# Attention values with column halves stationary, sinks as a score column, and a written TensorE order in the mixer

## The chip, the core and the metric
One core of a Trainium2 chip runs the whole program in one launch. The engines each have a queue of their own, executed in order: TensorE (PE; PEld is its load of the stationary operand), VectorE (DVE), ScalarE (ACT), GpSimd (POOL) and SyncE (SP, which issues most transfers). The metric is the device time of one execution in microseconds, the median over runs.

## What is computed
Two trunk layers over 384 tokens: 128 context tokens (block 0) and 256 latent tokens (blocks 1 and 2). A layer is a half-step SwiGLU, a mixer, and a second half-step SwiGLU. The mixer has four head groups behind one input projection: mLSTM, global attention (group B), windowed attention with sink logits (group C), and a Hyena long convolution; one output projection follows. The attention, cut from the reference:

```
def attn_probs(s, sink):
    if sink is None:
        return jax.nn.softmax(s, axis=-1)
    m = jnp.maximum(jnp.max(s, -1, keepdims=True), sink)
    e = jnp.exp(s - m)
    return e / (jnp.sum(e, -1, keepdims=True) + jnp.exp(sink - m))
...
    s = jnp.einsum('bqkgd,bmkd->bkgqm', qblk, k).astype(F32)
    p = attn_probs(s, sink)
    return jnp.einsum('bkgqm,bmkd->bqkgd', p.astype(v.dtype), v)
```

Each group has 4 query heads of 64 on 2 key heads (`kv`), two query heads (`g`) to a key head. Context queries see the 128 context keys, latent queries 128 cached keys and 256 of their own; group C masks the latent keys that lie further than 128 positions away and adds a sink logit to the softmax. The new context keys and values are outputs too.

## The kernel before
Activations lie feature-major (feature in the partition, 384 tokens in the free dimension). Every large product is exact to about float32 by three float32r matmuls (`prod3`, L235): high weights with high and low activations, low weights with high. Weights arrive by SP (`weights_load`, L219), ScalarE makes the high part (L231), VectorE the low one (L232), four buffers each. The order on each engine is chosen by the framework's planner from a cost model, by program order as priority; only the start of the kernel is written out (`manual_schedule`, L1391).

The mixer (L733) projects the mLSTM's queries and keys, then values, then group B and group C token-major (`tok_major`, L746), with the mLSTM's products between. Then comes the stage that the change touches:

- `attention(grp)` (L980): raw queries and keys are copied out of PSUM (L992), values too (L993). Per block in the order 1, 2, 0 they are normed (B, L1010 to L1012) or scaled (C, L1014 and L1015, on ScalarE), stored in `hat`, rotated (L1025 to L1027), transposed on TensorE (L1030) and copied to `qT` (L1031). `hat` of block 0 has one buffer (L1004) and is the source of the store of the new keys (L1017). The cached keys are transposed too (L999).
- `scores` (L1033): query block stationary, keys moving, the two key heads on partitions 0 to 63 and 64 to 127; cached and own keys are separate products; C adds a mask product in bfloat16 (L1053).
- softmax: maximum on VectorE (L1066), for C a minimum with the negated sink (L1068); exponential with its sum on ScalarE (L1070), for C another one for the sink (L1072) and an addition (L1073); reciprocal (L1074).
- the unnormalised probabilities are transposed (L1076), copied by VectorE (L1078), and are the stationary operand of the value product (L1083), with 64 columns of values moving. VectorE scales the result (L1084) into `ot`, which `to_cat` (L768) transposes back (L772) and splits into `ch` and `cl`, the high and low inputs of the output projection.
- `hyena_in` (L1110) makes three projections of 8 k-steps (24 matmuls) for each channel half m, then a short convolution on VectorE (L1131 to L1133). `hyena` (L1138) transposes (L1148), goes through a DFT (L594, L1159 to L1163) and back (L1169).
- the output projection (L1181): for each of two column halves q, four pairs of k-tiles, each with 4 x 2 x 3 matmuls.

In program order all of group B stands before group C, and that before Hyena; the planner moves Hyena's projections (`pdu`) forward into the attention. PSUM has two pools of four banks: `mm` for projections and `small` for the rest.

Of the kernel before, what the change touches and what calls it, by code (L numbers as in the profile page):

```python
# [9 lines left out]
F32 = mybir.dt.float32  # L10
# [7 lines left out]
P = 128  # L18
# [4 lines left out]
DEPTH = 2  # L23
# [67 lines left out]
def trunk_kernel(ctx: ExitStack, tc: tile.TileContext, I: dict, C: dict, O: list):  # L91
# [124 lines left out]
    def weights(src, nk, ncol, name):  # L216
        return weights_split(weights_load(src, nk, ncol, name), nk, ncol, name)

    def weights_load(src, nk, ncol, name):  # L219
# [485 lines left out]
    def mixer_constants():  # L705
# [12 lines left out]
        K["nsinks"] = const.tile([P, DEPTH, 4], F32, name="nsinks")  # L718
        tc.keep_in_program_order(V.tensor_scalar(out=K["nsinks"], in0=K["sinks"], scalar1=-1.0, scalar2=None, op0=ALU.mult))
# [13 lines left out]
    def mixer(l, K, nm, nxt, fill):  # L733
# [246 lines left out]
        def attention(grp):  # L980
            isB = grp == "B"
            pa = [mm(f"pa{b}") for b in range(3)]
            tok_major(pa, C_BQ if isB else C_CQ, f"{grp}{l}")
            kc = am.tile([P, 2 * HD], F32, tag="kc", name="kc")
            vc = am.tile([P, 2, HD], F32, tag="vc" + grp, name="vc")
            ksrc, vsrc = (I["cache_gattn_k"], I["cache_gattn_v"]) if isB else (I["cache_swa_k"], I["cache_swa_v"])
            nc.gpsimd.dma_start(out=kc, in_=ksrc[0, l].rearrange("t h d -> t (h d)"))
            nc.gpsimd.dma_start(out=vc, in_=vsrc[0, l])
            raw = [am.tile([P, 384], F32, tag="raw", bufs=3, name="raw") for b in range(3)]
            vt = am.tile([P, 3, 2, HD], F32, tag="vt" + grp, name="vt")  # L990
            for b in range(3):
                S.copy(raw[b], pa[b][:, 0:384])  # L992
                S.copy(vt[:, b], pa[b][:, 384:512].rearrange("p (h d) -> p h d", h=2))  # L993
            ko, vo = (5, 6) if isB else (7, 8)
            nc.scalar.dma_start(out=O[vo][0, l], in_=vt[:, 0])
            qT = am.tile([P, 3, NT], F32, tag="qT" + grp, name="qT")
            kcT = am.tile([P, P], F32, tag="kcT" + grp, name="kcT")
            pkc = small("pkc")
            T.transpose(pkc[:, :P], kc, ident)  # L999
            S.copy(kcT, pkc[:, :P])  # L1000
            if isB:
                rr = head_rstd(lambda b: raw[b], 6, "qn")
            for b in (1, 2, 0):
                hat = am.tile([P, 6, HD], F32, tag="hat" if b else "hat0", bufs=2 if b else 1, name="hat")  # L1004
                qv = hat[:, 0:4, :].rearrange("p (g kv) d -> p kv g d", g=2)
                rq = raw[b][:, 0:256].rearrange("p (kv g d) -> p kv g d", kv=2, g=2)
                rk = raw[b][:, 256:384].rearrange("p (h d) -> p h d", h=2)
                if isB:
                    rn = raw[b].rearrange("p (h d) -> p h d", h=6)
                    V.tensor_tensor(out=rn, in0=rn, in1=bc(rr[:, b, :].unsqueeze(2), [P, 6, HD]), op=ALU.mult)  # L1010
                    V.tensor_tensor(out=qv, in0=rq, in1=bc(K["gq"][:, l:l + 1, :].unsqueeze(1), [P, 2, 2, HD]), op=ALU.mult)
                    V.tensor_tensor(out=hat[:, 4:6, :], in0=rk, in1=bc(K["gk"][:, l:l + 1, :], [P, 2, HD]), op=ALU.mult)  # L1012
                else:
                    S.mul(qv, rq, 0.125)  # L1014
                    S.copy(hat[:, 4:6, :], rk)  # L1015
                if b == 0:
                    nc.gpsimd.dma_start(out=O[ko][0, l], in_=hat[:, 4:6, :])  # L1017
                else:
                    cosb = rope[:, b - 1, 0:1, :]
                    sinb = rope[:, b - 1, 1, :].rearrange("p (a h f) -> p a h f", a=2, h=2)  # L1020
                    t = am.tile([P, 6, HD], F32, tag="rt", bufs=2, name="rt")
                    hv = hat.rearrange("p n (a h f) -> p n a h f", a=2, h=2)
                    tv = t.rearrange("p n (a h f) -> p n a h f", a=2, h=2)
                    for hf in range(2):
                        V.tensor_tensor(out=tv[:, :, :, hf, :], in0=hv[:, :, :, 1 - hf, :], in1=bc(sinb[:, :, hf, :].unsqueeze(1), [P, 6, 2, 16]), op=ALU.mult)  # L1025
                    V.tensor_tensor(out=hat, in0=hat, in1=bc(cosb, [P, 6, HD]), op=ALU.mult)
                    V.tensor_tensor(out=hat, in0=hat, in1=t, op=ALU.add)  # L1027
                p = small("pqT")
                for j in range(3):
                    T.transpose(p[:, j * P:(j + 1) * P], hat[:, 2 * j:2 * j + 2, :].rearrange("p h d -> p (h d)"), ident)  # L1030
                S.copy(qT[:, :, b * P:(b + 1) * P], p[:, :NT].rearrange("p (j t) -> p j t", j=3))  # L1031
            ot = am.tile([P, 3, 256], F32, tag="ot", name="ot")
            def scores(b, g):  # L1033
                ss = [small("s") for _ in range(2)]

                def part(c0, n, key, start=True, stop=True):
                    for kv in range(2):
                        r = slice(kv * 64, kv * 64 + 64)
                        T.matmul(ss[kv][:, c0:c0 + n], lhsT=qT[r, g, b * P:(b + 1) * P], rhs=key(r), start=start, stop=stop)  # L1039

                own = lambda c0, n: (lambda r: qT[r, 2, c0:c0 + n])
                if b == 0:
                    part(0, P, own(0, P))
                    return ss
                part(0, P, lambda r: kcT[r, :])
                if isB:
                    part(P, 2 * P, own(P, 2 * P))
                    return ss
                near, far = (P, 2 * P) if b == 1 else (2 * P, P)
                part(near, P, own(near, P))  # L1050
                part(far, P, own(far, P), stop=False)
                for kv in range(2):
                    T.matmul(ss[kv][:, far:far + P], lhsT=K["ident16"], rhs=K["wmask"][:, (b - 1) * P:b * P], start=False, stop=True)  # L1053
                return ss

            for b in (1, 2, 0):
                nk = 1 if b == 0 else 3
                n = nk * P
                for g in range(2):
                    ss = scores(b, g)  # L1060
                    sts, pts = {}, {}
                    for kv, s in enumerate(ss):
# [4 lines left out]
                        if not isB:  # L1067
                            V.tensor_tensor(out=nmx, in0=nmx, in1=K["nsinks"][:, l, h:h + 1], op=ALU.min)  # L1068
# [411 lines left out]
```

## Time and profile before
| | us |
|---|---|
| median of three runs | 1672.38 |
| lowest and highest run | 1649.3, 1673.61 |
| the profiled execution | 1664.59 |
| its span, first to last instruction | 1662.8 |

The profile is of one execution: busy time and share of each engine, the span in 40 slices (a digit is a share in tenths, PEclk the TensorE clock granted by the throttle, in tenths of full speed), groups of instructions by line, waits, timelines. Times of a row count from the start of the span. A matmul's duration includes its way through the array, so that neighbours overlap; start to start says what one costs in a stream.

### The profile page before, as it was taken

The numbers are of one execution on the slowest core, as the hardware profiler recorded it, in microseconds if no ns is written. First come the engines' busy times: TensorE is split into PE (matmuls) and PEld (weight loads), VectorE is DVE, ScalarE is ACT, GpSimd is POOL, SyncE is SP. The second block draws the span as 40 slices with busy tenths as digits, with TensorE's granted clock in tenths as the row PEclk, the third lists the DMA queues.
The fourth block names the chain that finished last, engine by engine and source line by source line (L and its number), as shares of the span: only waits on it lengthen the run. The fifth ranks groups of instructions, "written<-read, shape, count | busy, mean of one in ns | idle before, by whom it ended". The sixth has DMA issues, their size and how long they took to land.

```text
span 1662.8 us, 25089 instructions
## 1 busy us (share of the span) xinstructions
PE 1621.3 (98%) x9145; PEld 1529.0 (92%) x9145; DVE 1272.1 (77%) x2564; ACT 761.0 (46%) x1771; POOL 240.9 (14%) x342
## 2 busy tenths in 40 slices
PE   7999999999989999999999999999999999999998
PEld 4789999997878999999999999999787899999997
DVE  5899997997858689996999977697785867444333
ACT  5534444458434464443546434345843446333331
POOL 2113222241010002221320211123101000000000
PEclk9999999999979999999999999999996999999999
DMA  9657757763431368766766774765343133444341
GB/s 309 203 156 244 225 183 242 220 179 104 128 63 59 102 189 242 240 185 199 216 207 192 240 210 135 243 211 146 103 131 59 53 108 115 127 127 127 114 133 58
DMA packets 235728, 271.23 MB, mean 163 GB/s; under 512 B 14239, under 2 KB 220287, under 8 KB 235604
## 3 DMA queue, kind: packets, MB, share of 16 engines
q1 hardware_dynamic: 223104, 248.67, 48.9%
q0 software_dynamic: 9472, 20.30, 4.9%
q10 hardware_dynamic: 3028, 0.64, 0.4%
q8 instruction: 72, 1.18, 0.3%
q14 instruction: 52, 0.43, 0.1%
HBM read 257.62 MB, written 3.57 MB: 157 GB/s over the span
## 4 chain that ended last, share of the span: by engine, by line
PE 75%; DVE 13%; issue 5%; DMA 4%; ACT 3%; POOL 0%; SPq 0%; DVEq 0%; ACTq 0%; POOLq 0%
PE pg L236 7%; PE pg L237 7%; PE pu L238 7%; PE pg L238 7%; PE pu L237 6%; PE pu L236 6%; DVE adacc L266 5%; PE pd L238 4%; PE pd L237 4%; PE pd L236 4%; PE s L1083 2%; PE s L1039 2%; PE pwo L238 1%; PE pwo L237 1%; PE pwo L236 1%
## 5 line engine op out<-in xcount | busy, mean ns | idle before, releaser
L266 DVE SCALAR_TENSOR_TENSOR adacc<-flat,sc,adacc 128x384 f32<-128x384 f32 (+1 forms) x602 | 353.0, 639 | 0.0
L290 POOL TENSOR_TENSOR adfold<-adacc,adfold 64x384 f32<-64x384 f32 (+1 forms) x86 | 122.3, 1422 | 149.2 <-DMA adfold<-adacc 146.8
L238 PE MATMUL pd<-ah,lo_db 128*128 128x384 f32 x352 | 119.2, 339 | 1.6 <-DVE lo_db L232 1.6
L238 PE MATMUL pd<-ah,lo_da 128*128 128x384 f32 x352 | 119.0, 338 | 1.7 <-DVE lo_da L232 1.7
L237 PE MATMUL pg<-wide,hi_gb 128*128 128x384 f32 (+1 forms) x352 | 119.6, 340 | 0.2
L236 PE MATMUL pg<-wide,hi_gb 128*128 128x384 f32 (+1 forms) x352 | 119.6, 341 | 0.0
L236 PE MATMUL pd<-ah,hi_da 128*128 128x384 f32 x352 | 119.5, 339 | 0.0
L236 PE MATMUL pd<-ah,hi_db 128*128 128x384 f32 x352 | 119.4, 339 | 0.0
L238 PE MATMUL pg<-wide,lo_gb 128*128 128x384 f32 (+1 forms) x352 | 118.9, 338 | 0.0
L237 PE MATMUL pd<-al,hi_db 128*128 128x384 f32 x352 | 118.9, 338 | 0.0
L237 PE MATMUL pu<-wide,hi_ub 128*128 128x384 f32 (+1 forms) x352 | 118.8, 338 | 0.0
L237 PE MATMUL pd<-al,hi_da 128*128 128x384 f32 x352 | 118.6, 337 | 0.0
L238 PE MATMUL pu<-wide,lo_ub 128*128 128x384 f32 (+1 forms) x352 | 118.5, 338 | 0.0
L236 PE MATMUL pu<-wide,hi_ub 128*128 128x384 f32 (+1 forms) x352 | 118.2, 337 | 0.0
L236 PE MATMUL pg<-wide,hi_ga 128*128 128x384 f32 (+1 forms) x328 | 112.8, 344 | 1.0 <-DVE sg L555 1.0
L236 PE MATMUL pu<-wide,hi_ua 128*128 128x384 f32 (+1 forms) x328 | 110.6, 338 | 2.7 <-DVE sg L555 2.7
L241 ACT CAST ah<-sg 128x384 fp32r<-128x384 f32 x88 | 45.2, 513 | 148.1 <-DVE sg L555 146.6
L237 PE MATMUL pg<-wide,hi_ga 128*128 128x384 f32 (+1 forms) x328 | 111.4, 340 | 0.0
L238 PE MATMUL pg<-wide,lo_ga 128*128 128x384 f32 (+1 forms) x328 | 111.3, 340 | 0.0
L237 PE MATMUL pu<-wide,hi_ua 128*128 128x384 f32 (+1 forms) x328 | 111.0, 338 | 0.0
L238 PE MATMUL pu<-wide,lo_ua 128*128 128x384 f32 (+1 forms) x328 | 110.8, 338 | 0.0
L232 DVE TENSOR_TENSOR lo_db<-st_db,hi_db 128x1024 fp32r<-128x1024 f32 (+1 forms) x48 | 54.4, 1133 | 64.2 <-ACT hi_db L231 64.2
(487 smaller groups left out, 4381.5 us busy)
## 6 DMA issues: line engine op xcount, KB each, us to landing
flat<-in_w_ada_dram SPq DMA_DIRECT2D x42, 1536.0 KB, 7.9
st_gb<-in_w_gate_dram SPq DMA_DIRECT2D x44, 512.0 KB, 3.8
st_ub<-in_w_up_dram SPq DMA_DIRECT2D x44, 512.0 KB, 4.7
st_ga<-in_w_gate_dram SPq DMA_DIRECT2D x41, 512.0 KB, 3.9
st_ua<-in_w_up_dram SPq DMA_DIRECT2D x41, 512.0 KB, 4.9
st_da<-in_w_down_dram SPq DMA_DIRECT2D x40, 512.0 KB, 5.3
st_db<-in_w_down_dram SPq DMA_DIRECT2D x40, 512.0 KB, 3.5
wst<-in_w_ada_dram SPq DMA_DIRECT2D x8, 1024.0 KB, 13.3
```

Source lines behind the costliest of these rows:

```text
L232: V.tensor_tensor(out=lo[:, :n], in0=st[:, :n], in1=hi[:, :n].bitcast(F32), op=ALU.subtract)]
L236: T.matmul(out, lhsT=lh, rhs=rh, start=start, stop=False)
L237: T.matmul(out, lhsT=lh, rhs=rl, start=False, stop=False)
L238: T.matmul(out, lhsT=ll, rhs=rh, start=False, stop=stop)
L241: S.copy(hi, src)
L266: last_step[0] = V.scalar_tensor_tensor(out=acc[:, s, :n * P], in0=w[:, k, :], scalar=sc[:, k, s:s + 1], in1=acc[:, s, :n * P], op0=ALU.mu ...
L290: G.tensor_tensor(out=fold[h, :c], in0=acc[h, s, :c], in1=fold[h, :c], op=ALU.add)
L1039: T.matmul(ss[kv][:, c0:c0 + n], lhsT=qT[r, g, b * P:(b + 1) * P], rhs=key(r), start=start, stop=stop)
L1083: T.matmul(s[:, NT:NT + HD], lhsT=pts[kv][:, j * P:(j + 1) * P], rhs=v, start=(j == 0), stop=(j == nk - 1))
```

## The change
The attention becomes a class `Group` with methods, and what TensorE executes from the last token-major projection to the end of the output projection stands in program order under `manual_schedule` for that engine alone; the other engines stay with the planner.

- Values: probabilities are normalised on ScalarE before they are transposed. The value product has 64 columns of values stationary and 128 columns of transposed probabilities moving; key head 0 writes the lower half of the output partitions, key head 1 the upper half. The result is feature-major, so `ot`, its scaling and `to_cat` of the two groups go; it is split at once. The rows of the output projection's weights for these groups are loaded in the order that this gives (`paired`, two transfers of 64 partitions).
- Sinks: one more column of the scores, made by a product of the identity with the sink column; maximum and sum then include it. `nsinks`, L1068, L1072 and L1073 go.
- Keys: queries, own keys and cached keys share one tile, so that a long step has one score product per key head instead of two or three. `hat` has three buffers for all blocks, and the context keys are stored from `ko` (B) or `raw` (C).
- Order: both groups are prepared first. Then a loop over 12 steps (group, block, query head) issues the scores of the next step, the transposes of this one, two k-steps of a Hyena projection (one for block 0), the values of this one, queries for four steps ahead, and again two k-steps. Hyena's first half runs inside these k-steps, its second half in fixed places of the output projection.
- Engines: of each pair of copies of probabilities one moves to ScalarE; so does the first term of the convolution.

```diff
-        nc.sync.dma_start(out=st[:, :n].rearrange("p (k f) -> p k f", k=nk), in_=src.rearrange("(k p) f -> p k f", p=P))
+        if paired:
+            for kv in range(2):
+                nc.sync.dma_start(out=out[kv * 64:kv * 64 + 64], in_=src.rearrange("(kv g d) f -> kv d g f", kv=2, g=2)[kv])
...
-                hat = am.tile([P, 6, HD], F32, tag="hat" if b else "hat0", bufs=2 if b else 1, name="hat")
+                    hat = am.tile([P, 6, HD], F32, tag="hat", bufs=3, name="hat")
...
+                    kh = hat[:, 4:6, :]
+                    if b == 0:
+                        kh = am.tile([P, 2, HD], F32, tag="ko", name="ko") if isB else rk
...
+            def queries(self, b):
+                p = mm("pqT")
...
+            def scores(self, b, g):
...
+                n = P if b == 0 else 3 * P
+                k0 = QW if b == 0 else QW + P
+                ss = [small("s") for _ in range(2)]
+                for kv in range(2):
+                    r = slice(kv * 64, kv * 64 + 64)
+                    T.matmul(ss[kv][:, 0:n], lhsT=qT[r, g * NT + b * P:g * NT + (b + 1) * P], rhs=qT[r, k0:k0 + n], start=True, stop=isB or b == 0)
+                if not isB:
...
+                    for kv in range(2):
+                        T.matmul(ss[kv][:, n:n + 1], lhsT=ident, rhs=K["sinks"][:, l, 2 * kv + g:2 * kv + g + 1], start=True, stop=True)
+                    n += 1
...
+                    V.tensor_reduce(out=nmx, in_=s[:, :n], axis=AX.X, op=ALU.max, negate=True)
+                    pe = am.tile([P, NT + 1], F32, tag="pe", bufs=2, name="pe")
+                    S.activation(out=pe[:, :n], in_=s[:, :n], func=AF.Exp, bias=nmx, accum_out=den)
+                    V.reciprocal(out=den, in_=den)
+                    n_ = P if b == 0 else 3 * P
+                    S.activation(out=pe[:, :n_], in_=pe[:, :n_], func=AF.Identity, scale=den)
...
+            def turned(self, b, ss, pes):
...
+                        T.transpose(ss[kv][:, j * P:(j + 1) * P], pes[kv][:, j * P:(j + 1) * P], ident)
+                    t = am.tile([P, NT], F32, tag="pts", bufs=2, name="pts")
+                    if kv:
+                        S.copy(t[:, :n], ss[kv][:, :n])
+                    else:
+                        V.tensor_copy(out=t[:, :n], in_=ss[kv][:, :n])
...
+            def valued(self, b, g, ss, pts):
+
+                vs = (self.vt[:, 0],) if b == 0 else (self.vt[:, 1], self.vt[:, 2], self.vc)
+                o = ss[0][:, NT:NT + P]
+                for j, v in enumerate(vs):
+                    for kv in range(2):
+                        T.matmul(o[kv * 64:kv * 64 + 64, :], lhsT=v[:, kv, :], rhs=pts[kv][:, j * P:(j + 1) * P], start=(j == 0), stop=(j == len(vs) - 1))
+                k = (2 if self.isB else 4) + g
+                split(o, ch[:, k, b * P:(b + 1) * P], cl[:, k, b * P:(b + 1) * P])
...
-                            T.matmul(s[:, NT:NT + HD], lhsT=pts[kv][:, j * P:(j + 1) * P], rhs=v, start=(j == 0), stop=(j == nk - 1))
-                        V.tensor_scalar(out=ot[:, b, h * HD:(h + 1) * HD], in0=s[:, NT:NT + HD], scalar1=sts[kv][:, 1:2], scalar2=None, op0=ALU.mult)
...
-        weave(attention("B"))
-        weave(attention("C"))
+        groups = [Group("B"), Group("C")]
...
-                V.tensor_scalar(out=o[:, 1:1 + n], in0=u[:, 1:1 + n], scalar1=cw(1), scalar2=col("conv_b", l * 6 + t6), op0=ALU.mult, op1=ALU.add)
+                S.activation(out=o[:, 1:1 + n], in_=u[:, 1:1 + n], func=AF.Identity, scale=cw(1), bias=col("conv_b", l * 6 + t6))
...
+        def filling():
+
+            yield from hyena_in(0, ucs[0])
+            first = hyena(0, ucs[0], mm)
+            for i, _ in enumerate(hyena_in(1, ucs[1])):
+                if i % 4 == 3:
+                    next(first, None)
+                yield
...
+        with tc.manual_schedule(engines={nc.tensor.engine}):
...
+            products(4)
+            inputs(0)
+            products(2)
+            inputs(2)
+            live = {0: groups[0].scores(*PAIRS[0])}
+            products(2)
+            for i, (gr, b, g) in enumerate(steps):
+                if i + 1 < len(steps):
+                    live[i + 1] = steps[i + 1][0].scores(*steps[i + 1][1:])
+                ss, pes = live.pop(i)
+                pts = gr.turned(b, ss, pes)
+                products(2 if b else 1)
+                gr.valued(b, g, ss, pts)
+                inputs(i + 4)
+                products(2 if b else 1)
...
+            last = hyena(1, ucs[1], small)
...
+                        if i < 3:
+                            next(last, None)
```

## Rows read from the trace of the kernel before
**Rows 1.** The page, busy shares and the span in 40 slices.
```profile
PE 1621.3 (98%) x9145; PEld 1529.0 (92%) x9145; DVE 1272.1 (77%) x2564; ACT 761.0 (46%) x1771; POOL 240.9 (14%) x342
...
PEclk9999999999979999999999999999996999999999
```
**Rows 2.** Stretches: us, busy PE, PEld, DVE, ACT, POOL; PEclk, DMA share, GB/s.
```profile
452.55:538.70 86.15, 81.56 (x506) 69.15 (x505) 62.35 (x195) 34.27 (x105) 9.37 (x32) 0.88 0.28 62
472.20:492.65 20.45, 20.45 (x83) 15.99 (x81) 8.85 (x26) 5.29 (x15) 0.00 (x0) 0.50 0.01 4
538.70:575.00 36.30, 36.30 (x212) 34.99 (x211) 22.77 (x46) 16.36 (x30) 0.00 (x0) 1.00 0.37 108
1241.95:1330.00 88.05, 84.34 (x506) 71.73 (x505) 62.34 (x195) 34.33 (x105) 9.38 (x32) 0.84 0.26 60
1260.65:1287.95 27.30, 27.30 (x106) 21.74 (x106) 11.53 (x39) 6.67 (x21) 0.00 (x0) 0.50 0.03 7
...
397.10:400.40 3.30, 3.30 (x9) 2.55 (x8) 2.91 (x8) 3.11 (x14) 1.33 (x3) 0.50 0.57 162
```
**Rows 3.** Waits of TensorE in each attention stage: total us, times, longest.
```profile
PE s L1076 <- ACT pe L1070: 4.5, 2, 3.8
...
PE s L1076 <- ACT pe L1070: 3.6, 2, 2.9
```
**Rows 4.** Timeline of ScalarE ahead of the fall: start, us, what, [idle before].
```profile
465.71 0.57 ACT L1070 ACTIVATE pe<-s,ast 128x384 f32<-128x384 f32 x1
...
470.68 0.42 ACT L1014 ACTIVATE hat<-raw 128x256 f32<-128x256 f32 x1 [4.30 <-DMA out_dram<-hat]
```
**Rows 5.** Timeline of TensorE in layer 0's attention stage.
```profile
452.55 0.33 PE L236 MATMUL pdu<-wide,hi_du 128*128 128x384 f32 x1
...
454.21 1.15 PE L973 MATMUL pc<-va,kw 128*64 128x65 f32 x16
...
456.04 0.34 PE L237 MATMUL pdu<-wide,hi_du 128*128 128x384 f32 x1
...
458.83 0.34 PE L238 MATMUL pdu<-wide,lo_du 128*128 128x384 f32 x1
...
460.84 0.49 PE L1030 MATMUL pqT<-ident,hat 128*128 128x128 f32 x3
...
461.35 0.34 PE L237 MATMUL pdu<-wide,hi_du 128*128 128x384 f32 x1
...
463.50 0.49 PE L1039 MATMUL s<-kcT,qT 64*128 64x128 f32 x4
463.83 0.69 PE L1039 MATMUL s<-qT 64*128 64x256 f32 x4
464.35 0.39 PE L1039 MATMUL s<-kcT,qT 64*128 64x128 f32 x4
...
505.41 0.33 PE L1083 MATMUL s<-vc,pts 128*128 128x64 f32 x2
505.57 0.61 PE L1083 MATMUL s<-vt,pts 128*128 128x64 f32 x4
...
506.25 0.33 PE L1083 MATMUL s<-vc,pts 128*128 128x64 f32 x2
```
**Rows 6.** Timeline of TensorE at the Hyena filter products (lower and upper output half).
```profile
82.52 0.85 PE L654 MATMUL fpsA<-feats,fw1c 34*64 34x384 f32 x2
...
84.57 0.81 PE L656 MATMUL fpsB<-feats,fw1f 34*64 34x384 f32 x2
85.30 0.45 PE L237 MATMUL pu<-wide,hi_ua 128*128 128x384 f32 x1
```
**Rows 7.** ScalarE by form in layer 0's stage: busy us, mean ns | idle before.
```profile
L231 ACT CAST hi_du<-st_du 128x1024 fp32r<-128x1024 f32 x3 | 3.1, 1050 | 3.9 <-PE pa L756 2.7 <-PE pdu L237 1.2
L1031 ACT COPY qT<-pqT 128x384 f32<-128x384 f32 x6 | 2.7, 487 | 0.9 <-PE pqT L1030 0.8
L993 ACT COPY vt<-pa 128x128 f32<-128x128 f32 x3 | 0.8, 276 | 0.0
```

More of the change, by code (lines that the diff above doesn't have):

```diff
@@ L977, in mixer @@
             nc.scalar.dma_start(out=O[3][0, l, d].rearrange("h (d o) -> d h o", o=1), in_=cs[:, :, HD:HD + 1], allow_slow_non_contiguous=True)
[L980 to L1003, printed above, removed]
-                hat = am.tile([P, 6, HD], F32, tag="hat" if b else "hat0", bufs=2 if b else 1, name="hat")
[L1005 to L1033, printed above, removed]
@@ L1041, in scores @@
[L1041 to L1051, printed above, removed]
-                for kv in range(2):
-                    T.matmul(ss[kv][:, far:far + P], lhsT=K["ident16"], rhs=K["wmask"][:, (b - 1) * P:b * P], start=False, stop=True)
@@ L1086, in attention @@
-            to_cat(ot, 2 if isB else 4)
-        def weave(*gens):
-            live = list(gens)
-            while live:
-                for g in list(live):
-                    if next(g, live) is live:
-                        live.remove(g)
-        weave(attention("B"))
-        weave(attention("C"))
+                        if b:
+                            far = P if b == 1 else 0
+                            T.matmul(ss[kv][:, far:far + P], lhsT=K["ident16"], rhs=K["wmask"][:, (b - 1) * P:b * P], start=False, stop=True)
@@ new lines, in mixer, with products, inputs @@
+        ucs = [{}, {}]
+        def filling():
[4 more added lines that the diff above has]
+                    next(first, None)
+                yield
+            for _ in first:
+                yield
+        between = filling()
+        def products(n):
+            for _ in range(n):
+                next(between, None)
+        with tc.manual_schedule(engines={nc.tensor.engine}):
+            steps = [(gr, b, g) for gr in groups for b, g in PAIRS]
+            ready = set()
+            def inputs(i):
+                if i < len(steps):
+                    gr, b, g = steps[i]
+                    if (gr, b) not in ready:
+                        ready.add((gr, b))
+                        if b == 1:
+                            gr.cached()
+                        gr.queries(b)
+            products(4)
[13 more added lines that the diff above has]
+                products(2 if b else 1)
+            for _ in between:
+                pass
+            last = hyena(1, ucs[1], small)
+            for q in range(2):
+                p = [mm(f"pwo{m}") for m in range(4)]
+                for i, k0 in enumerate((0, 2, 4, 6)):
+                    w_src = I["w_out"][l][k0 * P:(k0 + 2) * P, q * 512:(q + 1) * 512]
+                    w = weights(w_src, 2, 512, f"wo{l}{q}{k0}", paired=k0 in (2, 4))
+                    for m in range(4):
+                        for k in range(2):
+                            prod3(p[m][:, :NT], w[0][:, k, m * P:(m + 1) * P], w[1][:, k, m * P:(m + 1) * P], ch[:, k0 + k, :], cl[:, k0 + k, :],
+                                  i == 0 and k == 0, i == 3 and k == 1)
+                        if i < 3:
+                            next(last, None)
+                for m in range(4):
+                    resid(4 * q + m, p[m], l, 5)
+                    nxt.prep(4 * q + m)
```

149 lines of the change are left out of this document (86 added, 63 removed).

## Prediction
> **What bounds the kernel now.** I read the page's busy shares first: TensorE is busy 98% of the span [rows 1], so only what shortens its own stream, or its waits, can count. The PEclk line of the same page dips near a quarter and three quarters of the span [rows 1]: the two mixers. The busy time by stretch then gives the place. From the end of group C's projection to the first output product, layer 0 takes 86.15 us and layer 1 88.05 us, at a mean granted clock of 0.88 and 0.84 [rows 2]. [...]
>
> The waits of TensorE say what stood ahead of each fall: transposes of probabilities wait for ScalarE's exponentials, 4.5 and 3.6 us, the longest 3.8 and 2.9 us [rows 3]. ScalarE's timeline names the cause. It finishes an exponential at about 466.3 us and then idles 4.30 us for a DMA, the store of group B's context keys (`out_dram<-hat`), because group C's `hat` of block 0 wants the same single buffer [rows 4]. The next exponentials stand behind that instruction in ScalarE's queue, TensorE waits for them, and as it starts again the clock is at half. In the half-clock stretches TensorE is busy throughout [rows 2], but with small work at half speed.
>
> **What the stage costs without waits.** I price TensorE by starts, not durations, since matmuls overlap. A projection matmul (384 columns): 16 of them take 458.83 - 456.04 = 2.79 us, 0.174 us each. A transpose: three and one projection matmul take 461.35 - 460.84 = 0.51 us, so 0.112 each. A value instruction: six and one projection matmul take 506.25 - 505.41 = 0.84 us, so 0.111 each. Scores: four 128-column instructions take 463.83 - 463.50 = 0.33 us, four of 256 columns 464.35 - 463.83 = 0.52 us; two heads on the two row halves share that time. The state products take 1.14 us. All these are from [rows 5].
>
> Counts per layer come from the code: 144 projection matmuls (25.1 us), 97 transposes (10.9), 56 value products of two instructions each (12.4), scores of B 4 x 0.85 + 2 x 0.33 = 4.1 and of C 14 x 0.33 = 4.6, state products 1.1, Hyena's 20 + 12 instructions about 4.6 (0.11 for 128 columns, 0.22 for 256), masks 0.5 (8 at half a transpose). Sum 63.3 us. So 23 to 25 us of each stage are idle time, half clock and waits too short for the profile to list.
>
> **The change, part by part.** *Values.* The counts stay; the stationary side becomes 64 columns and the moving side 128. Upper bound: nothing overlaps, 12 x 0.111 = 1.33 us for a long step, as now. Lower bound: the two heads, which write the lower and the upper half of the output, run side by side, six slots and one, 7 x 0.111 = 0.78 us. The nearest row is of this kind: 12 filter instructions of 384 columns, six for each output half, take 85.30 - 82.52 = 2.78 us [rows 6], where one after another they would take 12 x 0.32 = 3.8 (estimate: 384 columns at 0.11 per 128). I take 0.78: 8 x 0.55 + 4 x 0.11 = 4.8 us less per layer; bound, none. Changing between the whole array and a split one costs up to 85.30 - 84.57 - 2 x 0.32 = 0.09 us a border [rows 6]; twelve value groups have two borders each, 2.2 us; bound, none.
> *Sinks.* 24 instructions of one column behind a 128-column load are new. Bounds 0.07 us (the 16 state products in 1.14 us) and 0.112 (transposes, [rows 5]); I take 0.112, also 128 stationary columns: 2.7 us.
> *Removed and merged.* 12 output transposes, 1.3 us. One score product of 384 columns for 128 + 256 or for three of 128: 0.33, 0.52, so 0.71 us, against 0.85 and 0.99, 4 x 0.14 + 4 x 0.28 = 1.7 us less; bound, none.
> Net: -4.8 + 2.2 + 2.7 - 1.3 - 1.7 = -2.9 us, bounds -6.1 and +3.6. Work per layer becomes 60.4 us.
>
> *The DMA wait.* The keys are now stored from `ko` or from `raw`, and `hat` has three buffers. The 4.5 and 3.6 us go. What is late next is the reuse of `hat`: group C's blocks wait for TensorE's transposes of group B's, the third of them one step into the loop, but C is needed only after six steps.
>
> *The written order.* Every dependent burst is followed by two k-steps of the Hyena projection (six matmuls, 1.04 us), and scores run one step ahead. A long step holds scores 0.71, transposes 0.67, values 0.78 with borders 0.18, queries about 0.18, and twelve projection matmuls 2.09: 4.6 us in B, 5.2 in C with sink and mask. From a step's scores to its transposes TensorE has about that long. The softmax fits: two exponentials of 0.57 [rows 4], two scalings at the 0.49 of a copy [rows 7], VectorE's maximum before, about 3 us. The copy of probabilities, 0.49 us, has 1.04 us of cover; without it each step would pay the copy and its signals, about 0.7 us. I allow 0.4 us a step for work queued ahead of these on ScalarE or VectorE, 4.8 us per layer.
>
> *The start.* Here the order loses something. Before the first query transpose stand only four k-steps (2.1 us) and the mLSTM tail (0.7 + 1.1): 452.55 + 3.9 = 456.5 us, while the rotated queries came by 460.84. The planner's order had 33 projection matmuls in between, from 452.55 on [rows 5]; the written one has 12. Nothing can pass a waiting instruction on TensorE. Idle up to 4.3 us; I take 4, plus 1.6 for the second block, the copy of the queries and the first softmax. That is as long as the waits that preceded the falls of the clock [rows 3], so I let it fall once more. For how long is bounded by the stretch at 397.10, 3.3 us at half clock with full-width matmuls behind one another, and by 27.30 [rows 2]. Projections now make up nearly half of each step, so I take twice the short one, 6.6 us: 3.3 us lost.
>
> *At no cost.* Four more half-size loads per layer on SP, hidden by a DMA share of 0.28 in the stage [rows 2]; were one late, the 24 output products of its k would wait behind it. ScalarE takes over scaling, half of the copies and the convolution's first term, hidden as long as it keeps below TensorE's step (a rival). VectorE loses as much as it gains, POOL nothing. The last Hyena part, in fixed slots of the output projection, may wait for VectorE: I take 1 us per layer.
>
> Sum: 60.4 + 4.8 + 5.6 + 3.3 + 1 = 75.1 us in place of 86.15 and 88.05: 11.0 + 13.0 = 24.0 us less. From the profiled execution's 1664.6 us (span 1662.8 and 1.8 around it) that is 1640.6. That execution lies inside the three runs shown (1649.3 to 1673.6), 0.5% under their median of 1672.4.
>
> **Rivals.** *The start closes too.* If two subtractions of weights (some 1.2 us each) move behind the rotations in VectorE's queue, the idle falls by 2.4 us, the clock holds (3.3 us) and a step waits 0.1 us instead of 0.4 (3.6 us): 9.3 us per layer, 1622. For it: the output projection's stream runs at full clock with Hyena's last products in it [rows 2]. Against: where VectorE puts them is still the planner's choice.
> *ScalarE paces the loop.* Per long step two exponentials 1.14 [rows 4], two scalings 0.98, copies of probabilities 0.49, split 0.28, queries 0.24, and half of a projection's cast, copies and convolution term, (1.05 + 0.66 + 0.49)/2 = 1.1: 4.2 us [rows 7] of 4.6. It decides from 0.4 us of disorder a step. With steps of 5.9 us, 8 x 1.3 less 3.2 already allowed is 7.2 us per layer: 1655.
> *Values do not pair.* Both halves stream through the same rows; if that serialises them, 4.8 us per layer return: 1650. The filter rows speak against it [rows 6]. [...]
> *The other side: the clock stays low.* If the start drops the clock and the loop never raises it, the stage is 2 x 60.4 + 5.6 = 126 us and the time 1664.6 + 40 + 38 = 1743. Break-even: without its clock loss the new stage is 71.8 us, so 2 x (87.1 - 71.8) = 31 us at half clock per layer; 2% slower needs 64 us. The longest stretch so far, 27.30 us [rows 2], is below both.
> [...]
>
> **How the numbers follow.** Forecast 0.42, its own range 1629 to 1652; the 1622 case 0.31; ScalarE (1648 to 1666) 0.15; no pairs 0.06; low clock 0.06. Two per cent, about what a measurement of this kernel can tell from no change, is 33 us: faster means under 1631. That takes nearly all of the 1622 case and a seventh of the forecast: 0.36. Slower is the low clock: 0.06. The rest, 0.58, lies within. The range 1612 to 1662 leaves out the low clock, the far ends of ScalarE and of the 1622 case, 0.16 together.
>
> **What would show it.** Right: no ScalarE wait on `out_dram<-hat`; both stages near 75 us; no half-clock stretch over 7 us; one TensorE wait of about 4 us at the first query transposes; the two heads' value instructions starting within one slot of each other; long steps of about 5 us. Wrong: half clock that lasts through the loop, TensorE waiting for ScalarE in every step, or stages that shrink without the total.

## Result, and the profile after

The changed kernel takes 1684.81 us (median of 4, 1679.83 to 1690.72), the kernel before, run beside it, 1664.16 us. The ratio is 1.0121, 95% interval 1.0071 to 1.0171: slower by about 1.2%, within 2%. The prediction was 1640.6 us, range 1612 to 1662. It is wrong, and in its direction.

The profiled execution has a span of 1682.1 us, 19.3 more than before. 17.5 of them lie in the two attention stages, 1.3 ahead of layer 0's and 0.5 behind layer 1's. The windows of the changed kernel, from the first Hyena projection to the first output product of layer 0 and of layer 1, and a short stretch and the output projection of layer 0 (columns: window, its length, busy time of PE, PEld, DVE, ACT and POOL, mean granted clock, DMA share, GB/s):

```profile
453.80:548.80 95.00, 76.72 (x472) 57.49 (x471) 51.24 (x143) 51.33 (x143) 8.77 (x31) 0.91 0.26 59
...
490.70:494.10 3.40, 3.40 (x15) 2.74 (x14) 0.52 (x3) 0.75 (x3) 0.00 (x0) 0.50 0.02 5
1252.10:1348.80 96.70, 79.38 (x471) 60.11 (x470) 51.12 (x141) 51.41 (x142) 8.79 (x31) 0.86 0.26 58
...
548.80:588.00 39.20, 39.07 (x227) 37.53 (x226) 23.81 (x49) 17.50 (x33) 0.00 (x0) 1.00 0.32 96
```

The stages were 86.15 and 88.05 us [rows 2] and are 95.0 and 96.7. The output projection of layer 0, from its first product to the next SwiGLU's first, takes 39.4 us before (538.72 to 578.12) and 39.5 after (548.77 to 588.32). TensorE was busy for 81.56 of 86.15 us [rows 2]; now it is busy for 76.72 of 95.00. Less what the half clock adds, by the mean granted clock, that is an estimated 71 and 68 us. So it has a little less to do, and it waits. For what, TensorE's waits in layer 0's stage say (columns: what waited, for what, us in total, times, longest):

```profile
PE s L1101 <- DVE pts L1091: 6.4, 5, 2.0
PE s L1101 <- ACT pts L1089: 4.7, 6, 1.5
PE pkc L1048 <- ACT vt L1003: 2.2, 1, 2.2
PE s L1086 <- ACT pe L1077: 2.0, 1, 2.0
PE s L1059 <- ACT qT L1044: 1.4, 1, 1.4
PE pqT L1043 <- ACT qT L1049: 1.0, 1, 1.0
PE pqT L1043 <- DVE hat L1037: 0.4, 1, 0.4
```

The two largest are new, 11.1 us: the value products (L1101) wait for the copies of the transposed probabilities, one made by VectorE (L1091), one by ScalarE (L1089). One step shows why. TensorE's timeline (columns: start, duration, what, in brackets the idle time before it and what ended it):

```profile
484.66 0.92 PE L1059 MATMUL s<-qT 64*128 64x384 f32 x4
485.51 0.87 PE L1086 MATMUL s<-ident,pe 128*128 128x128 f32 x6
486.14 0.42 PE L242 MATMUL pdu<-wide,hi_du 128*128 128x384 f32 x1
...
487.10 0.33 PE L244 MATMUL pdu<-wide,lo_du 128*128 128x384 f32 x1
489.40 0.68 PE L1101 MATMUL s<-pts,vt 128*64 128x128 f32 x7 [1.97 <-DVE pts L1091]
```

Scores of step i+1, transposes of step i, two k-steps of the Hyena projection, then 1.97 us of nothing. The transposes are issued by 486.1. VectorE's timeline of the same stretch:

```profile
485.61 0.56 DVE L1072 TENSOR_REDUCE ast<-s 128x1 f32<-128x384 f32 x1 [1.49 <-PE s L1059]
486.08 1.21 DVE L238 TENSOR_TENSOR lo_du<-st_du,hi_du 128x1024 fp32r<-128x1024 f32 x1
487.21 0.61 DVE L1138 SCALAR_TENSOR_TENSOR uc<-hu,colsm,uc 128x385 f32<-128x385 f32 x1
487.75 0.15 DVE L1075 RECIPROCAL ast<-ast 128x1 f32<-128x1 f32 x1
487.82 0.53 DVE L1072 TENSOR_REDUCE ast<-s 128x1 f32<-128x384 f32 x1
488.27 0.60 DVE L1139 SCALAR_TENSOR_TENSOR uc<-hu,colsm,uc 128x385 f32<-128x385 f32 x1
488.80 0.55 DVE L1091 COPY pts<-s 128x384 f32<-128x384 f32 x1
```

The copy that TensorE wants stands last, some 2.7 us after the transposes. Ahead of it are both maxima of the next step (L1072), a subtraction of weights and two convolution terms, none of which TensorE needs now. ScalarE's timeline of the step before has the same order, with both exponentials (L1074) and both scalings (L1077) of the next step ahead of its copy:

```profile
479.95 0.58 ACT L1074 ACTIVATE pe<-s,ast 128x384 f32<-128x384 f32 x1 [1.87 <-DVE ast L1072]
...
480.53 0.57 ACT L1074 ACTIVATE pe<-s,ast 128x384 f32<-128x384 f32 x1
...
481.08 1.11 ACT L1077 ACTIVATE pe<-pe,ast 128x384 f32<-128x384 f32 x2
482.09 0.47 ACT L1089 COPY pts<-s 128x384 f32<-128x384 f32 x1
```

TensorE's order is written out; those of VectorE and ScalarE are still the planner's. From the transposes of layer 0's first step to those of its twelfth pass 76.5 us (470.4 to 546.9). Of the eight long steps six take 6.2 to 8.8 us, one 5.1, and one with the last Hyena products 11.3.

### The profile page after: what moved, and what is told of

Read it like the earlier page. It is cut to its first block, busy times and chain, and to the rows that moved or that the text cites. A ratio compares the mean times of both kernels' runs of the same rounds, so it can differ in the third digit from the quotient of the medians.

```text
span 1682.1 us, 24889 instructions
## 1 busy us (share of the span) xinstructions
PE 1612.4 (96%) x9073; PEld 1507.1 (90%) x9073; DVE 1247.4 (74%) x2447; ACT 794.3 (47%) x1845; POOL 239.0 (14%) x342
## 4 chain that ended last, share of the span: by engine, by line
PE 76%; DVE 15%; ACT 4%; DMA 2%; issue 2%; SPq 0%; DVEq 0%; ACTq 0%
PE pg L242 7%; PE pg L244 7%; PE pu L244 7%; PE pg L243 7%; PE pu L243 7%; PE pu L242 7%; DVE adacc L272 5%; PE pd L244 4%; PE pd L242 4%; PE pd L243 4%; PE pwo L242 1%; PE pwo L244 1%; PE pwo L243 1%; PE s L1101 1%; PE pa L760 1%
```

## Experiments

The letters of the theories are not those of the attention groups. My theory (A): the order of VectorE's and ScalarE's queues makes the copies late. The late copy holds back the values, the values hold back the freeing of the score banks and so the next scores, and each step becomes a ring. Rivals: (B) ScalarE simply has too much to do (51.33 us busy in the stage after, 34.27 before); (D) the new forms of values, sinks and scaling cost more than priced. For the prediction's own first step there is one more question: was the wait for the store worth what I gave it?

All times are medians; the kernel before, timed beside these runs, had medians of 1667.3 to 1670.1 us. The stages are those of one profiled execution each, in us.

| run | us | ratio to before, 95% | stage, layer 0 and 1 |
|---|---|---|---|
| changed kernel | 1684.8 | 1.0071 to 1.0171 | 95.0, 96.7 |
| e1, copies first | 1648.9 | 0.9832 to 0.9956 | 77.4, 76.3 |
| e2, kernel before, `hat` alone | 1637.8 | 0.9782 to 0.9880 | 73.2, 72.9 |
| e3, TensorE by the planner | 1644.3 | 0.9822 to 0.9920 | 75.1, 74.9 |
| e4, ScalarE relieved | 1673.0 | 1.0013 to 1.0074 | 89.3, 91.1 |
| e5, e1 with another start | 1651.7 | 0.9853 to 0.9931 | 78.5, 78.5 |
| e6, e1 and e4 | 1658.7 | 0.9916 to 0.9976 | 83.4, 83.2 |
| e7, transposes ahead of scores | 1655.3 | 0.9877 to 0.9967 | 80.3, 79.1 |
| e8, more cover | 1679.7 | 1.0046 to 1.0091 | 93.8, 92.9 |
| e9, e1 with late rotations | 1640.8 | 0.9785 to 0.9925 | 73.5, 74.2 |
| e10, e9 with another start | 1651.2 | 0.9888 to 0.9947 | 77.7, 77.8 |
| e11, e9, TensorE by the planner | 1646.6 | 0.9832 to 0.9950 | 74.7, 74.6 |

**Copies first (e1).** TensorE's order stays; `scores` is cut in two, and the softmax of step i+1 is queued behind both copies of step i.

```
-                    live[i + 1] = steps[i + 1][0].scores(*steps[i + 1][1:])
+                    nx, nb, ng = steps[i + 1]
+                    nss = nx.scores(nb, ng)
                 ss, pes = live.pop(i)
                 pts = gr.turned(b, ss, pes)
+                if i + 1 < len(steps):
+                    with tc.issue_after(copied[-2].ins), tc.issue_after(copied[-1].ins):
+                        live[i + 1] = (nss, nx.softmax(nb, nss))
```

> Theory A (queue order): in the changed kernel the copies of a step's transposed probabilities stand on VectorE and ScalarE behind the next step's maxima, exponentials and scalings, and TensorE waits for them before the value products (listed in layer 0's stage: 6.4 + 4.7 us, and 8.2 + 6.7 us at the weight loads). Here TensorE's order is as in the changed kernel, and only the softmax of step i+1 is queued behind both copies of step i. A expects those waits to fall below a third, a long step to go from 6.3 to 7.9 us towards 5, and the stage from 95.0 and 96.7 us towards 80 to 86: 1655 to 1668 us in all against 1685. Theory B (ScalarE's load paces the loop, 51.3 us busy in the stage against 34.3 before): the load is the same, so the time stays at 1680 to 1690. Theory D (sinks, split values and borders cost more than priced): the same, 1680 to 1690.

1648.9 us, 36 less than the changed kernel and below A's range. Nothing was taken out and no load was moved. The window of its stage in layer 1:

```profile
1237.00:1313.30 76.30, 67.68 (x470) 51.26 (x469) 51.23 (x141) 50.17 (x142) 8.80 (x31) 1.00 0.32 73
```

TensorE's timeline of one step in it:

```profile
1257.63 1.30 PE L1059 MATMUL s<-qT 64*128 64x384 f32 x4
1258.86 0.87 PE L1089 MATMUL s<-ident,pe 128*128 128x128 f32 x6
1259.49 0.42 PE L242 MATMUL pdu<-wide,hi_du 128*128 128x384 f32 x1
...
1260.73 0.66 PE L1104 MATMUL s<-pts,vt 128*64 128x128 f32 x8
```

VectorE's timeline of that step, first the copy of step i, then the maxima of step i+1:

```profile
1259.45 0.56 DVE L1094 COPY pts<-s 128x384 f32<-128x384 f32 x1 [1.48 <-PE s L1089]
1259.92 1.01 DVE L1075 TENSOR_REDUCE ast<-s 128x1 f32<-128x384 f32 x2
```

And ScalarE's, the copy and then the first exponential:

```profile
1259.77 0.48 ACT L1092 COPY pts<-s 128x384 f32<-128x384 f32 x1 [1.75 <-PE s L1089]
1260.57 0.58 ACT L1077 ACTIVATE pe<-s,ast 128x384 f32<-128x384 f32 x1 [0.31 <-DVE ast L1075]
```

Both copies now begin as soon as the transposes are there. TensorE goes through the step without a wait, and the granted clock is 1.00 (0.86 in the changed kernel's layer 1). Of TensorE's waits for copies, 11.1 us in the changed kernel, 0.8 are left in either layer:

```profile
PE s L1104 <- DVE pts L1094: 0.8, 2, 0.6
```

From the first step's transposes to the twelfth's pass 59.0 us in place of 76.5. ScalarE is as busy as before, 50.2 us, and no longer in the way.

**Two lines exchanged (e7).** The transposes of step i are issued ahead of the scores of step i+1; no queue is pinned.

```
-                if i + 1 < len(steps):
-                    live[i + 1] = steps[i + 1][0].scores(*steps[i + 1][1:])
                 ss, pes = live.pop(i)
                 pts = gr.turned(b, ss, pes)
+                if i + 1 < len(steps):
+                    live[i + 1] = steps[i + 1][0].scores(*steps[i + 1][1:])
```

> The changed kernel with two lines exchanged: a step's probabilities are transposed before the next step's scores are issued, and no queue is pinned. The copies then have their input first and the planner puts them ahead of the next softmax. Theory A expects the waits before the values to go; the next step's transposes then have behind the scores only four k-steps and the values, about 2.1 + 0.8 us, to cover a softmax of some 3.9 us (two maxima 1.0, exponentials 0.77 each, two scalings), so a long step of 5.2 to 5.8 us: 1653 to 1668 us. If the order of the two queues is not what counts: 1680 us or more.

1655.3 us, 29 less than the changed kernel. VectorE's timeline of a step in layer 0 now has the copy ahead of the maxima:

```profile
483.55 0.56 DVE L1091 COPY pts<-s 128x384 f32<-128x384 f32 x1 [0.27 <-PE s L1086]
...
485.26 0.55 DVE L1072 TENSOR_REDUCE ast<-s 128x1 f32<-128x384 f32 x1
```

TensorE has no listed wait for a copy left in that stage. The written order had issued the scores of the next step just ahead of this step's transposes, and with that order the planner's queues had the next softmax first.

**More cover (e8).** Four k-steps between the transposes and the values, none behind.

```
-                products(2 if b else 1)
+                products(4 if b else 2)
                 gr.valued(b, g, ss, pts)
                 inputs(i + 4)
-                products(2 if b else 1)
```

> The changed kernel with all four k-steps of a step between its transposes and its values, none behind them: 1.04 us more cover for the copies, whose waits were 1 to 2.4 us. If only cover was short, 0.6 to 1.0 us of each of 16 long steps goes: 1669 to 1676 us. If the late copy closes a ring (copy, values, banks, scores, softmax, copy), what is gained ahead of the values is lost ahead of the next scores: 1680 to 1692 us.

1679.7 us, 5 less, a difference that the overlapping intervals leave open, and between the two expectations. TensorE's waits in layer 0's stage show the ring:

```profile
PE s L1059 <- DVE wide L248: 7.3, 5, 2.6
...
PE s L1101 <- ACT pts L1089: 1.1, 2, 0.9
```

The waits for the copies fall from 11.1 to 1.1 us, as cover should make them. In their place the next scores wait 7.3 us until VectorE has split the values and a bank is free. Cover moved the wait along the ring; the order of the queues (e1, e7) took it away.

**ScalarE relieved (e4).** Scalings and the convolution's first term on VectorE.

```
-                    S.activation(out=pe[:, :n_], in_=pe[:, :n_], func=AF.Identity, scale=den)
+                    V.tensor_scalar(out=pe[:, :n_], in0=pe[:, :n_], scalar1=den, scalar2=None, op0=ALU.mult)
...
-                S.activation(out=o[:, 1:1 + n], in_=u[:, 1:1 + n], func=AF.Identity, scale=cw(1), bias=col("conv_b", l * 6 + t6))
+                V.tensor_scalar(out=o[:, 1:1 + n], in0=u[:, 1:1 + n], scalar1=cw(1), scalar2=col("conv_b", l * 6 + t6), op0=ALU.mult, op1=ALU.add)
```

> The changed kernel with the scaling of the probabilities (24 instructions a layer of 0.4 to 0.6 us) and the convolution's first term (6 of 0.71 us) on VectorE instead of ScalarE. Theory B (ScalarE paces) expects ScalarE's busy time in the stage to fall from 51 to about 35 us, as before the change, and the time with it by 10 to 16 us a layer: 1655 to 1668 us. Theory A expects no gain worth the name, since the copies still stand behind the next step's softmax, now with scalings ahead of them on VectorE: 1677 to 1695 us.

1673.0 us: 12 less than the changed kernel, neither A's "no gain" nor B's 17 to 30.

```profile
456.00:545.30 89.30, 73.42 (x470) 54.96 (x469) 59.84 (x170) 37.64 (x113) 8.90 (x31) 0.94 0.28 62
```

ScalarE's load is down to 37.6 us and the stage is still 89.3 us, far from the 77.4 of e1. TensorE's waits for ScalarE's copies are down from 4.7 to 1.5 us, those for VectorE's stay, 6.8 us. By itself this run left B open, so the same edit was made with the copies first (e6).

> The copies-first kernel with the scaling and the convolution's first term on VectorE as well. Alone, relieving ScalarE gave some 12 us. Theory B as a cause of its own expects the same here: 1635 to 1640 us. Theory A says that ScalarE's load counted only because it stood ahead of late copies: with the copies first, nothing is gained, 1645 to 1655 us.

1658.7 us, 10 more than e1. VectorE is busy for 60.3 us of layer 0's stage (51.3 in e1), TensorE waits 2.3 us for its copies (0.8), and the mean granted clock is 0.90 (0.98), over the whole run 0.984 (0.992). With the copies in time the relief of ScalarE only loads VectorE, and costs. B is not a cause of its own: ScalarE's work counted where it stood ahead of a late copy.

**One part of the change alone (e2).** The kernel before, with three `hat` buffers in turn and the stored keys of block 0 out of a tile of their own or out of `raw`.

```
-                hat = am.tile([P, 6, HD], F32, tag="hat" if b else "hat0", bufs=2 if b else 1, name="hat")
+                hat = am.tile([P, 6, HD], F32, tag="hat", bufs=3, name="hat")
...
+                kh = hat[:, 4:6, :]
+                if b == 0:
+                    kh = am.tile([P, 2, HD], F32, tag="ko", name="ko") if isB else rk
...
-                    nc.gpsimd.dma_start(out=O[ko][0, l], in_=hat[:, 4:6, :])
+                    nc.gpsimd.dma_start(out=O[ko][0, l], in_=kh)
```

> The kernel before with one part of the change: three buffers of hat in turn and the stored keys of block 0 taken from a tile of their own or from raw, so that no engine waits for their store. As the prediction has it, the wait of 4.3 us on that store brings waits of 4.5 and 3.6 us to TensorE, and the half-clock stretches of 20.45 and 27.30 us follow from them: without them both layers lose the wait and most of the half clock, 10 to 17 us a layer, 1630 to 1645 us against 1664. If the half clock comes from the thin work of the loop itself, only the waits go: 1653 to 1658 us. If the exponentials wait for something else by then: 1660 to 1666 us.

1637.8 us, 31.5 less than the kernel before beside it, and the fastest run of the study. The stages:

```profile
454.10:527.30 73.20, 72.11 (x507) 61.94 (x506) 62.42 (x196) 34.15 (x104) 9.40 (x32) 1.00 0.30 73
1230.00:1302.90 72.90, 72.10 (x506) 61.96 (x505) 62.30 (x196) 34.12 (x104) 9.41 (x32) 1.00 0.31 74
```

13.0 and 15.2 us a layer went with one wait of 4.3 us [rows 4], which is not among ScalarE's waits any more, and the granted clock of both stages is 1.00 (0.88 and 0.84 before [rows 2]). The prediction's first step holds. The changed kernel has this part in it and takes 47 us more, so the rest of the change cost that much.

**TensorE by the planner (e3).** The changed kernel without `manual_schedule`.

> The changed kernel without the written TensorE order: the planner orders TensorE too, with the other engines' queues; values, sinks, scores and copies are those of the changed kernel. Theory A expects the planner to move other work of TensorE ahead where a copy is late, and the time to come out under the changed kernel's 1685 us, at 1650 to 1675. Theory D (the new forms of values, sinks and scaling are what cost) expects 1680 us or more, with the work of TensorE in the stage up by the same amount as in the changed kernel.

1644.3 us, 40 less than the changed kernel, below A's range. The new forms are all in it, so (D) falls as the main cause. What it leaves open is small: against e2, with the same freedom of TensorE's order, the new forms come out 6.5 us behind, where the sum had them 6 ahead. In layer 0's stage TensorE is busy for 71.7 us (72.1 in e2) and has 3.3 us of listed waits (1.0).

**The start (e5, e9, e10).** In e1 TensorE still waits about 6 us between the first key transpose and the first turned step. e5 gave the first transposes other banks and put 12 k-steps instead of 8 ahead of the loop.

> The kernel of the copies-first run with another start: the first transposes of keys and queries take banks of the small pool, which are free by then, instead of waiting for ScalarE's copy out of a bank of the projection (2.1 us in layer 1 of that run), and 12 k-steps of the Hyena projection instead of 8 stand ahead of the loop, four fewer in group B's steps behind the values. The waits of TensorE from the first key transpose to the first turned step add up to 6.4 us there (2.1, 1.1, 0.4, 1.1, 0.7, 1.0). If the bank and the thin start are their cause, 3 to 5 us a layer go: 1639 to 1643 us against 1649. If the rotated queries are late in any order, the wait only moves to the query transposes and 1 to 2 us a layer go: 1645 to 1647.

1651.7 us, a miss: the waits at the start fell to 4.2 us, but the loop lacked the k-steps, and one step of group B took 7.26 us where it had taken 5.32. TensorE's timeline of its start shows the longest of them:

```profile
463.77 0.55 PE L1043 MATMUL pqT<-ident,hat 128*128 128x128 f32 x3
...
466.19 0.92 PE L1059 MATMUL s<-qT 64*128 64x384 f32 x4 [1.88 <-ACT qT L1044]
```

ScalarE's timeline has the copy that it waited for:

```profile
465.63 0.51 ACT L1044 COPY qT<-pqT 128x384 f32<-128x384 f32 x1
```

VectorE's has the first maxima, and what stood ahead of them:

```profile
467.98 0.55 DVE L1037 TENSOR_TENSOR hat<-hat,rt 128x384 f32<-128x384 f32 x1
468.45 0.61 DVE L1142 SCALAR_TENSOR_TENSOR uc<-hu,colsm,uc 128x385 f32<-128x385 f32 x1
468.98 1.01 DVE L1075 TENSOR_REDUCE ast<-s 128x1 f32<-128x384 f32 x2
```

Queue order again. The queries are transposed by 464.3, but ScalarE copies them at 465.63; the first maxima come at 468.98, some 2 us after their scores, behind rotations of group C, which are wanted six steps later. So e9 is e1 with these rotations in the loop's first three steps.

```
+                if i < 3:
+                    with tc.issue_after(copied[-2].ins), tc.issue_after(copied[-1].ins):
+                        groups[1].rotate((1, 2, 0)[i])
                 inputs(i + 4)
```

> The copies-first kernel with the same treatment of the start: the rotations of group C's queries, which are wanted only from the seventh step on, are queued in the loop's first three steps behind the copies of those steps. In the run with the other start VectorE began the first maximum 2 us after its scores, behind rotations of group C, and ScalarE's copies of the queries stood behind group C's scalings. If queue order is what holds the start back too, 2 to 3.5 us a layer go: 1642 to 1645 us against 1649. If VectorE has no room for the rotations in the loop, what the start gains is lost there: 1648 us or more.

1640.8 us, 8 less than e1, and a little below the expected range; stages of 73.5 and 74.2 us. The two were timed in different sets of runs, but their runs do not overlap (1637.8 to 1642.0, 1644.3 to 1651.3). e10 then tried the other start once more on top of it.

> The same, with the first transposes in banks of the small pool and 11 k-steps ahead of the loop instead of 8 (6, 3 and 2 for 4, 2 and 2), which the last step then lacks. If the start is thin and not only out of order, 1 to 3 us a layer more go: 1637 to 1642 us. If k-steps moved to the start are missed in the loop, as in the run with the other start: no less than the kernel with late rotations alone.

1651.2 us, a second miss. What the start took is missing at the end, where TensorE has nothing to do while the last softmax runs. Its timeline there, in layer 1:

```profile
1311.23 0.44 PE L1110 MATMUL s<-pts,vt 128*64 128x128 f32 x4
1314.49 0.63 PE L1095 MATMUL s<-ident,pe 128*128 128x128 f32 x2 [2.83 <-ACT pe L1086]
1315.20 0.96 PE L1110 MATMUL s<-pts,vt 128*64 128x128 f32 x4
1316.09 0.69 PE L242 MATMUL pwo<-wide,hi_wo 128*128 128x384 f32 x1
```

The wait of 2.83 us is 0.40 at that place in e9. Behind it the first 2 us of the output projection are at a granted clock of 0.50, with matmuls that start 0.32 us apart (1316.58 to 1316.90) as in the changed kernel's stretch at 0.50 (491.31 to 491.63), and the whole of it is at 0.97, where it is at 1.00 in e9. The 48 k-steps are a fixed supply of cover; those ahead of the loop are taken from it. Last, e9 with TensorE in the planner's hands (e11):

> The kernel with late rotations and the copies first, but TensorE ordered by the planner and not in the written order. The planner's order without these pins gave 1644 us. If late copies cost there too: 1636 to 1641 us. If the planner had already put other work of TensorE where a copy is late: 1642 to 1646 us.

1646.6 us against 1644.3 in e3: pins bring nothing there. The written order needs them, the planned one does not. e2 and e9 both beat both kernels; between the two, 1636.6 to 1639.2 and 1637.8 to 1642.0 us in two sets of runs, this study does not decide. No run with the new forms came out below e2, so a gain of theirs over the buffers alone is not shown.

## Why the prediction was wrong, point by point

**What bound the kernel: right.** The wait for the store, and the half clock after it, were worth 31.5 us (e2), 13.0 and 15.2 us by stage. The prediction's rows give about that: 4.5 and 3.6 us of waits, and half of 20.45 and 27.30 us, some 15 and 17 us.

**The loop: the step that failed.** I wrote that the copy of probabilities "has 1.04 us of cover" and allowed 0.4 us a step "for work queued ahead of these". I had looked at how long the copy takes, and not at what stands ahead of it. The allowance was 4.8 us a layer; the waits for copies alone are 11.1. The prediction named the price without cover as 0.7 us a step, which was also too little, since in the step shown the copy is behind 3.2 us of VectorE's work (485.61 to 488.80), not merely exposed.

**The clock: mis-sized, as a consequence.** I gave the half clock 6.6 us a layer. By the mean granted clock of 0.91 and 0.86 it is an estimated 17 and 27 us, (1 - 0.91) x 2 x 95.0 and (1 - 0.86) x 2 x 96.7, with 0.50 and 1.00 as the two values, as in the listed stretches; so 8.6 and 13.5 us are lost instead of 3.3. Alone this would not have made the kernel slower, since I had put the break-even at 31 us of half clock a layer. The row at 490.70 stands right behind the wait of 1.97 us. In e1 the clock is 0.98 and 1.00.

**TensorE's work: priced short in both kernels.** I had 63.3 us before and 60.4 after. At full clock and nearly without waits, TensorE is busy 72.1 us with the old forms (e2); with the new ones 67.4 in the written order (e9's layer 0) and 71.7 in the planner's (e3's). Starts that I read off undisturbed rows leave out what lies between unlike instructions: in e1 a projection matmul behind the values takes 0.28 us to the next start (1298.61 to 1298.89), where a stream has 0.174. The difference is 4.7 or 0.4 us less, by the order, where I had 2.9, and within the bounds given. But the error does not cancel in the sum: a priced stage of 75.1 us stood there against measured ones of 86.15 and 88.05. It also made me read 23 to 25 us of each stage as removable, where e2 shows 13 to 15.

**Added up for layer 0.** Listed waits 7.0 at the start and 11.1 for copies, clock 8.6, work about 68: 94.7 of 95.0 us. Forecast were 5.6, 4.8, 3.3 and 60.4 + 1. Of the 19.9 us between 75.1 and 95.0, then, the work makes some 6.7, the copies 6.3, the clock 5.3 and the start 1.4. With the work and the start alone put right in both layers the sum would be an estimated 1657 us, still in the range; the late copies, and the clock that fell with them, take it out.

**The start: right in size, half right in cause.** 7.0 us against 5.6 in layer 0. Of the 4 us that I gave the rotated queries 0.4 is listed; in e5, where no bank holds the transposes back, it is 1.8. 2.2 us is a wait for a bank of the projection, which `pkc` and `pqT` now share with `pa` and `pdu`, and part is the queue order that e9 undoes.

**Values: right.** The halves pair. TensorE's groups by line in layer 1's stage, the value products of e2, in the old form (columns: busy time, mean ns of one, idle time before them):

```profile
L1087 PE MATMUL s<-vt,pts 128*128 128x64 f32 x80 | 12.6, 272 | 0.0
...
L1087 PE MATMUL s<-vc,pts 128*128 128x64 f32 x32 | 5.7, 260 | 0.0
```

The same of e1, in the new form:

```profile
L1104 PE MATMUL s<-pts,vt 128*64 128x128 f32 x80 | 7.3, 288 | 0.8 <-DVE pts L1094 0.8
...
L1104 PE MATMUL s<-pts,vc 128*64 128x128 f32 x32 | 3.1, 273 | 0.0
```

Each instruction takes about as long as before, but 112 of them fill 10.4 us instead of 18.3. Part of that is the order around them: in e3, in the planner's order, 108 of the new form fill 13.7. By starts, the twelve of a long step take 0.80 us in e1's layer 1, where the old form took 1.33 [rows 5] and 0.78 was forecast, as TensorE's timeline shows from the first product to the matmul behind them:

```profile
1297.81 0.66 PE L1104 MATMUL s<-pts,vt 128*64 128x128 f32 x8
...
1298.61 0.44 PE L242 MATMUL pdu<-wide,hi_du 128*128 128x384 f32 x1
```

By starts the two halves are 1.66 times as fast as the old form, 1.33 to 0.80 us.

**Smaller terms.** Four sinks take 0.42 us in e1 (1295.54 to 1295.96, by starts, in layer 1; forecast 0.45). Scores of a long step take 0.85 us (484.66 to 485.51 above), not 0.71: merging brought nothing in group B. In group C it is 0.85 us as well (1294.57 to 1295.42 in e1), 0.14 less than before, half of what I had. The output projection is 0.1 us longer than it was in layer 0, so the 1 us allowed for its last Hyena part, and the loads at no cost, were enough.

**The rivals.** The time came out above all of them but the low clock. "ScalarE paces the loop" had the right symptom and a point of decision, 0.4 us of disorder a step, that was passed; its reason, the load, falls with e6. I had put no mechanism on the slower side but a clock that stays low. The one that happened, a late copy on VectorE, was in the text as a cover and not as a rival.

**The range.** 1612 to 1662 missed 1684.8. e9, where the queues are in order, gives 1640.8, so the sum was about that of a kernel whose other two engines follow the written order as well. That the two agree so closely is luck: in e9's layer 0 the work is 67.4 us and not 60.4, while the waits for copies are 0.6 us and not 4.8, and no half clock stands where I had 3.3 us.

## What to carry to other kernels

An order written for one engine is only half an order. Before pricing it, go through each instruction that this engine will wait for, and ask what stands ahead of it in its own engine's queue: here it was work of the next step that became ready earlier. If the producer's queue is left to a planner, either pin it, or issue the step so that the wanted input is ready first (e7: two lines). And where a short wait precedes a long stretch at half clock, test the removal of the wait alone first; here a new buffer rotation gained 31.5 us, and the whole change as it was built lost some 20.

## What the runs showed of the hardware

The scatter of the kernel before goes with its clock. Over its 33 runs beside e1 to e8 it took 1649.7 us at the highest mean granted clock of the whole run, 0.991, and 1674.3 at one of the lowest, 0.975; 0.016 of 1670 us are 27 us, about that difference. e2, whose stages stay at full clock, lies between 1636.6 and 1639.2 us in its four runs. So part of the gain from removing the wait seems to be a narrower spread, which one profile doesn't show.

Splitting the array in column halves cost little at its borders. In e1's layer 1 the time by starts from the last projection matmul ahead of a value group (1297.54) to the second one behind it (1298.89) is 1.35 us; less two of 0.174, 1.00 us is left for twelve products and both borders, against 1.33 us for twelve in the old form [rows 5]. The products themselves take 0.80 us of it, so some 0.2 us are the two borders, which is about the 0.18 forecast. Behind the transposes ahead of them, which use the whole array, the first projection matmul takes 0.26 us to the next start as well (1296.57 to 1296.83), so that the split itself need not be what costs them.
